# A float32 two-block network on one core: wide projections, features by transposes, low parts by accumulating transfers, attention rows late

## The chip, the cores and the metric

The kernel runs on one core of one Trainium2 chip. Its metric is the device time of one execution in microseconds (us). The engines are named as in the profile: PE (matmuls), PEld (the loading of PE's stationary operand), DVE (elementwise and reductions), ACT (activations and copies), POOL (general purpose; here it could issue transfers) and SP, whose queue issues almost every transfer.

## The reference, cut to what matters

The input is 256 positions of width 1024, float32. The first block has two layers; the second block has two more.

```python
# first block, layer 0: mLSTM mixer, then conv FFN; layer 1: attention, then conv FFN
u = rmsnorm(x, norm_g) @ w_in;  q, k, v, o, gates = split(u)
h = h + (rmsnorm(mlstm(q, k, v, gates)) * sigmoid(o)) @ w_out      # a_w_out
u = rmsnorm(h, g) @ w_up;  c = causal_conv3(u);  val, gate = split(c)
h = h + (silu(gate) * val) @ w_down
h = h + attention(q from h, k and v shared) @ w_o                  # b_w_o
# second block, twice
h = rmsnorm(x, g_pre) * (1 + scale) + shift
u_val, u_gate, g_conv, c_q, c_kv, k_idx, w_idx, g_attn = split(h @ w_in)
y_conv = (silu(layernorm(causal_conv31(u_val * sigmoid(u_gate)))) @ w_pw2) * silu(g_conv)
y_attn = top_k_attention(c_q, c_kv, k_idx, w_idx) * silu(g_attn)
x = x + gate * rmsnorm(concat(y_conv, y_attn) @ w_out, g_post)
```

## The kernel before, in words

Activations lie feature-major in the first block (128 features on the partitions, 256 positions along the row) and row-major in the second block's residual `hm` (two halves of 128 positions, index `t`). Most products are made of high and low parts, both in pages of the kernel's type `F32R`, the high one rounded to it. `split_w` (L525) makes a weight page's high part by a copy on ACT and its low part by a subtraction on DVE. `mm3` (L565) then adds three products: high by high, high by low, low by high. A weight page is 128 x 1024 values, 512 KB; a `Chunk` (L533) is one or two pages. A chunk named in `NATIVE` (L92) is not split: its matmuls run in full float32, which the trace shows as two records each.

`gemm_pair` (L632) computes 256 output features by 256 positions from a chunk of eight slices: 2 x 8 x 3 matmuls of 256 columns. `gemm_sums` (L592) does the same from operands whose high and low parts lie side by side in one page ("rr"): per slice one 512-column product of the weights' high part with both, and one 256-column product of the weights' low part with the high part (`mm2`, L582). The two halves of the PSUM bank are then added. Before the change only the FFN's up projections, from the third chunk on, use it.

The second block's features come from `Head` (L1096). `norm(t)` makes the row statistics and scales the identity matrix by them; `feats(t)` multiplies the rows by that matrix, which scales and transposes them in one full-float32 matmul. ACT evicts eight blocks from PSUM with scale and shift, and ACT and DVE split them.

A layer of the second block (`dsa_layer`, L1186) takes the latents (456 columns), the index scores, the top-k choice (DVE), the four convolution projections `u`, 30 taps on DVE, queries, gates (`w_ga`, `w_gc`), eight heads, then the output rows: `acc` holds the rows of both halves, first the attention's four slices for both halves, then `w_pw2`, then the convolution's four slices, the rest of the norm and the next layer's features, half by half.

The order on every engine is written ahead of time by a planner (`Program.order`, L193). It goes by the order of the program text as priority, with an estimate for each instruction, and lets an engine take a later instruction while an earlier one is not ready. Pages are limited: 24 of type R (split parts), 25 of type F (raw weights and float32 data). An instruction is placed when its pages are free, so the prefetch runs as far ahead as pages allow. An accumulating transfer would be issued by POOL, plain loads by SP; each queue keeps its order.

Of the kernel before, what the change touches and what calls it, by code (L numbers as in the profile page):

```python
# [41 lines left out]
for _n, _c in CONSTS:  # L42
# [5 lines left out]
PAGES = {  # L48
    "R": (1024, F32R, 24),
    "F": (1024, F32, 25),  # L50
    "s": (16, F32, 40),
# [334 lines left out]
def build(ctx, tc, a):  # L386
# [137 lines left out]

    def split_w(raw, n):  # L525
        hi, lo = new("w", n), new("w", n)
        op = act(hi, raw, AF.Copy)
        if hold[0]:
            pg.after(op, hold[0])
        tt(lo, raw, hi.f32, ALU.subtract)  # L530
        return hi, lo

    class Chunk:  # L533


        def __init__(self, dram, kc, mc, k0=0, native=False, cuts=None):
            self.mc, self.kp, self.k0 = mc, 1024 // mc, k0
            self.parts = []
            for k in range(k0, kc, self.kp):
                n = min(self.kp, kc - k) * mc  # L540
                raw = new("raw", n)
                if cuts:
                    hi, lo = new("w", n), new("w", n)
                    for c in cut(cuts, n):
                        load(raw[:, c], dram[:, k * mc + c.start:k * mc + c.stop])
                        act(hi[:, c], raw[:, c], AF.Copy)
                        tt(lo[:, c], raw[:, c], hi[:, c].f32, ALU.subtract)
                    self.parts.append((hi, lo))
                    continue
                load(raw, dram[:, k * mc:k * mc + n])  # L550
                self.parts.append((raw, None) if native else split_w(raw, n))

# [29 lines left out]
    def mm2(out, pairs, start, stop):  # L582
# [6 lines left out]
        pg.add("PE", 2 * (768 / 2.4 + 6), emit, [x for (lh, ll), both in pairs for x in (lh, ll, both)], [out])  # L589


    def gemm_sums(ch, both):  # L592
        out = []
        for b in range(2):
            ps, lo, u = psum(), blk(), blk()
            for k in range(0, 8, 2):
                mm2(ps, [(ch.at(i, b * 128, b * 128 + 128), both[i]) for i in (k, k + 1)], k == 0, k == 6)
            act(lo, ps[:, 256:512], AF.Copy)
            tt(u, ps[:, 0:256], lo, ALU.add)
            out.append(u)  # L600
        return out
# [36 lines left out]
    def half(ps, b):  # L638
        return ps[:, b * S:b * S + S]
# [32 lines left out]

    def scaled(xs, gname, i0):
        out = []
        for k, x in enumerate(xs):
            hi, lo = new("r"), new("r")
# [13 lines left out]


    xs = scaled(xT, None, 0)
# [133 lines left out]
    for j in range(2):  # L826
# [9 lines left out]
        for i in range(2):  # L836
            tp = psum()
            for b in range(2):
                for t in range(2):
                    tr(tp[:, b * S + t * 128:b * S + t * 128 + 128], yt[t * 2 + i][:, b * 128:b * 128 + 128], ident)  # L840
            for b in range(2):
                m, yh, yl = 4 * j + 2 * i + b, new("r"), new("r")
                act(yh, half(tp, b), AF.Copy, scale=ghalf[:, m:m + 1])
                stt(yl, half(tp, b), ghalf[:, m:m + 1], yh.f32, ALU.mult, ALU.subtract)
                ys.append((yh, yl))
# [208 lines left out]
    for h in range(8):  # L1054
        op = psum()
        c = slice((h % 4) * 128, (h % 4) * 128 + 128)
        mm(op[:, 0:256], vt[h // 4][0][:, c], pTs[h][:, 0:256], True, False)
        mm(op[:, 128:256], vt[h // 4][1][:, c], pTs[h][:, 256:384], False, True)
        ys.append(split_x(op[:, 0:256]))
    proj_res("b_w_o", ys, xT)  # L1060


# [33 lines left out]
    class Head:  # L1096
# [89 lines left out]
    def dsa_layer(l, h, last):  # L1186
        hd, xs = heads[l], heads[l].xs
        lw = Chunk(a["w_lat"][l], 8, 456)
        lat = [psum() for _ in range(2)]
# [31 lines left out]
        hold[0] = None  # L1221
        ch = Chunk(a["w_qidx"][l], 2, 512)
        qix = []
# [36 lines left out]
        for j in range(4):  # L1260
            ps = gemm_pair(Chunk(a["w_u"][l * 4 + j], 8, 256, 0, f"u{j}" in NATIVE), xs)
            th, u2, y = blk(), blk(), blk()
# [32 lines left out]
        hold[0] = None  # L1295
        ch = Chunk(a["w_uq"][l], 2, 1024)
        qs = []
# [11 lines left out]
        def gate(i):  # L1309
            nme, j = ("w_ga", "w_gc")[i // 2], i % 2  # L1310
            ps = gemm_pair(Chunk(a[nme][l * 2 + j], 8, 256, 0, f"{nme}{j}" in NATIVE), xs)
            for b in range(2):
# [52 lines left out]
        ch = Chunk(a["w_pw2"][l], 4, 512, 0, "pw" in NATIVE)  # L1365
        for j in range(2):
# [8 lines left out]
        chs = [Chunk(a["w_out_2"][l * 8 + k], 1, 1024, 0, "oc" in NATIVE) for k in range(4)]  # L1375
# [134 lines left out]
```

## Time and profile before

| | us |
|---|---|
| median of three runs | 857.73 (857.71 to 860.17) |
| the profiled execution | 860.24 |
| its span | 858.4 |
| PE busy in the span | 847.8 |

The span is from the first to the last instruction of the profiled execution; 1.8 us of its time lie around the span. A line in the profile names source line, engine, operation, and what is written from what; line 439 is ACT's helper for all activations, 452, 457 and 463 are DVE's, 426 and 430 are plain matmuls and transposes on PE, 573 to 575 the three products of `mm3`, 585 and 587 the two kinds of `mm2`.

### The profile page before, as it was taken

How to read it: one execution, taken by the hardware profiler on the slowest of the kernel's cores; microseconds unless marked ns; L12 is line 12 of the kernel's file. 1: busy time of each engine (PE TensorE's matmuls, PEld its weight loads, DVE VectorE, ACT ScalarE, POOL GpSimd, SP SyncE). 2: the span in 40 equal slices, each digit the busy share in tenths (PEclk: the TensorE clock that was granted, in tenths of full speed). 3: DMA queues.
4: the chain of work that ended last, by engine and by line, in shares of the span. 5: the costliest groups of instructions: out<-in, count | busy, mean ns of one | idle time of the engine just before them, and what ended most of it. 6: DMA issues, size and time to landing. Idle time of an engine off the chain costs nothing.

```text
span 858.4 us, 14510 instructions
## 1 busy us (share of the span) xinstructions
PE 847.8 (99%) x5182; PEld 744.0 (87%) x5182; DVE 751.8 (88%) x1712; ACT 586.5 (68%) x1234; POOL 0.2 (0%) x4
## 2 busy tenths in 40 slices
PE   8999999999999999999999999999999999999997
PEld 8988998999998988889988888888998857998866
DVE  6756899999999899986999999886799998799895
ACT  6845577766666597774787766666953887953883
POOL 0000000000000000000000000000000000000000
PEclk9999999999999999999999999999999999999999
DMA  8985864978877645477377888652430157440201
GB/s 315 408 328 195 295 209 141 316 267 279 263 251 251 198 149 172 142 262 287 123 275 262 297 269 272 195 162 72 162 124 14 52 213 295 133 144 14 59 16 49
DMA packets 50407, 170.19 MB, mean 198 GB/s; under 512 B 5860, under 2 KB 8436, under 8 KB 50336
## 3 DMA queue, kind: packets, MB, share of 16 engines
q1 hardware_dynamic: 50192, 169.28, 57.8%
q8 instruction: 40, 0.66, 0.3%
q14 instruction: 31, 0.25, 0.1%
q10 hardware_dynamic: 144, 0.00, 0.0%
HBM read 167.89 MB, written 1.37 MB: 197 GB/s over the span
## 4 chain that ended last, share of the span: by engine, by line
PE 94%; DVE 3%; ACT 1%; DMA 1%; issue 0%; SPq 0%; DVEq 0%; ACTq 0%
PE ps L573 18%; PE ps L574 17%; PE ps L575 17%; PE ps L585 17%; PE ps L426 14%; PE ps L587 8%; PE ps L430 2%; DVE R L452 2%; DVE F L457 1%; ACT F L439 1%; PE ps L608 1%; DMA F<-in_a_w_v_dram 1%; DVE F L452 0%; PE ps L1276 0%; ACT R L439 0%
## 5 line engine op out<-in xcount | busy, mean ns | idle before, releaser
L452 DVE TENSOR_TENSOR R<-F,R 128x1024 fp32r<-128x1024 f32 (+4 forms) x339 | 325.4, 986 | 24.7 <-ACT R L439 22.2
L573 PE MATMUL ps<-R,R 128*128 128x256 f32 (+3 forms) x1004 | 324.7, 323 | 1.3 <-ACT R L439 1.2
L574 PE MATMUL ps<-R,R 128*128 128x256 f32 (+3 forms) x1004 | 316.8, 316 | 1.3 <-DVE R L452 1.0
L575 PE MATMUL ps<-R,R 128*128 128x256 f32 (+3 forms) x1004 | 316.5, 315 | 0.0
L439 ACT ACTIVATE R<-F 128x1024 fp32r<-128x1024 f32 (+4 forms) x339 | 284.6, 863 | 21.9 <-DVE F L452 16.9
L573 PEld LDWEIGHTS ps<-R,R 128*128 128x128 f32 x1004 | 192.3, 192 | 14.7 <-ACT R L439 2.6
L574 PEld LDWEIGHTS ps<-R,R 128*128 128x128 f32 x1004 | 192.5, 192 | 12.7 <-DVE R L452 2.9
L575 PEld LDWEIGHTS ps<-R,R 128*128 128x128 f32 x1004 | 192.3, 192 | 12.0 <-DVE R L452 0.8
L585 PE MATMUL ps<-R,R 128*128 128x512 f32 x640 | 201.2, 396 | 0.0
L439 ACT ACTIVATE F<-ps 128x256 f32<-128x256 f32 (+4 forms) x269 | 99.9, 393 | 111.6 <-PE ps L587 39.5
L457 DVE SCALAR_TENSOR_TENSOR F<-F,par,F 128x255 f32<-128x255 f32 (+11 forms) x346 | 143.7, 470 | 2.1 <-ACT F L439 1.5
L587 PEld LDWEIGHTS ps<-R,R 128*128 128x128 f32 x640 | 120.1, 188 | 28.7 <-DVE R L452 0.7
L426 PE MATMUL ps<-F,F 128*128 128x256 f32 (+6 forms) x566 | 127.2, 376 | 0.9 <-ACT F L439 0.7
L587 PE MATMUL ps<-R,R 128*128 128x256 f32 x640 | 126.0, 278 | 0.0
L426 PEld LDWEIGHTS ps<-F,F 128*128 128x128 f32 (+2 forms) x566 | 90.1, 190 | 19.6 <-issue 8.2
L585 PEld LDWEIGHTS ps<-R,R 128*128 128x128 f32 x640 | 98.7, 189 | 1.3
L452 DVE TENSOR_TENSOR F<-ps,F 128x256 f32<-128x256 f32 (+2 forms) x152 | 63.6, 432 | 30.6 <-ACT F L439 14.6
L439 ACT ACTIVATE F<-F 128x256 f32<-128x256 f32 (+2 forms) x112 | 43.7, 413 | 47.5 <-DVE F L457 41.1
L457 DVE SCALAR_TENSOR_TENSOR F<-F,F 128x1024 f32<-128x1024 f32 (+1 forms) x53 | 60.3, 1146 | 6.7 <-ACT F L439 6.7
L439 ACT ACTIVATE F<-F,par 128x256 f32<-128x256 f32 x96 | 57.0, 595 | 8.0 <-DVE F L452 7.1
L457 DVE SCALAR_TENSOR_TENSOR F<-F,par 128x255 f32<-128x255 f32 (+1 forms) x86 | 41.0, 480 | 1.0 <-ACT F L439 0.7
L439 ACT ACTIVATE F<-F,s 128x128 f32<-128x128 f32 (+1 forms) x80 | 33.2, 444 | 4.1 <-DVE s L478 3.3
(99 smaller groups left out, 421.9 us busy)
## 6 DMA issues: line engine op xcount, KB each, us to landing
F<-in_f_w_up_dram SPq DMA_DIRECT2D x88, 512.0 KB, 5.3
F<-in_w_ada_dram SPq DMA_DIRECT2D x48, 512.0 KB, 5.0
F<-in_f_w_down_dram SPq DMA_DIRECT2D x44, 512.0 KB, 4.6
F<-in_w_u_dram SPq DMA_DIRECT2D x16, 512.0 KB, 5.2
F<-in_w_out_dram SPq DMA_DIRECT2D x16, 512.0 KB, 3.5
F<-in_a_w_o_dram SPq DMA_DIRECT2D x8, 512.0 KB, 10.1
F<-in_a_w_out_dram SPq DMA_DIRECT2D x8, 512.0 KB, 10.2
F<-in_w_k_dram SPq DMA_DIRECT2D x8, 512.0 KB, 4.6
```

The lines of the kernel that those rows point to most:

```text
L426: pg.add("PE", dur, lambda: nc.tensor.matmul(g(out), g(lhsT), g(rhs), start=start, stop=stop, skip_group_check=not check), [lhsT, rhs], [out])
L430: pg.add("PE", 110.0, lambda: nc.tensor.transpose(g(out), g(x), g(idn)), [x, idn], [out])
L439: nc.scalar.activation(g(out), g(x), func, bias=g(bias), scale=g(scale), **kw)
L452: return pg.add("DVE", ddur(n or x.n), lambda: nc.vector.tensor_tensor(g(out), g(x), g(y), op), [x, y], [out])
L457: nc.vector.scalar_tensor_tensor(g(out), g(x), g(s), g(y), op0, op1, **kw)
L573: nc.tensor.matmul(o, g(lh), g(rh), start=start, stop=False, **kw)
L574: nc.tensor.matmul(o, g(lh), g(rl), start=False, stop=False, **kw)
L575: nc.tensor.matmul(o, g(ll), g(rh), start=False, stop=stop, **kw)
L585: nc.tensor.matmul(g(out), g(lh), g(both), start=start and i == 0, stop=False, skip_group_check=True)
L587: nc.tensor.matmul(g(out[:, 0:256]), g(ll), g(both[:, 0:256]), start=False, stop=stop and i == 1, skip_group_check=True)
L608: nc.tensor.matmul(g(out[e * 64:e * 64 + 64, c]), g(v[s][e]), g(p[e][:, r]), start=s == 0, stop=s == 1, skip_group_check=True)
```

## The change

Pages: R from 24 to 27, F from 25 to 22. The query chunks, the second key chunk and both output projections use the wide form; their operands are made side by side, and an output projection adds both halves of each bank to the residual. `norm` scales the rows themselves in three pieces on DVE, and `feats` transposes them. In the second block `w_gc1` is no longer native, and for `w_gc1`, `pw`, `w_ga0`, `w_gc0` and `u2` the low part is a negated copy of the high part by ACT, to which a transfer issued by POOL adds the raw page. The attention's output rows of the second half stand behind the first half's rows. Gates 2 and 3 are computed one pair of heads earlier. (Adapted calls of `Chunk` are left out below.)

```diff
-    "R": (1024, F32R, 24),
-    "F": (1024, F32, 25),
+    "R": (1024, F32R, 27),
+    "F": (1024, F32, 22),
...
-GATES = (0, 1), (), (2,), (3,), ()
+HSCALE = (0, 256, "D"), (256, 512, "D"), (512, 1024, "D")
+GATES = (0, 1), (2,), (3,), (), ()
...
-NATIVE = {"oa", "u3", "w_ga1", "w_gc1"}
+NATIVE = {"oa", "u3", "w_ga1"}
+BY_DMA = {"w_gc1", "pw", "w_ga0", "w_gc0", "u2"}
+ACCTAIL = 6000.0
...
-    def split_w(raw, n):
+    def split_w(raw, n, by_dma=False):
         hi, lo = new("w", n), new("w", n)
         op = act(hi, raw, AF.Copy)
...
-        tt(lo, raw, hi.f32, ALU.subtract)
+        if by_dma:
+            act(lo, hi.f32, AF.Copy, scale=-1.0)
+            pg.add("POOL", 1100.0, lambda: nc.gpsimd.dma_start(g(lo), g(raw), accum_op=ALU.add), [raw, lo], [lo], tail=ACCTAIL)
+        else:
+            tt(lo, raw, hi.f32, ALU.subtract)
...
+    def gemm_wide(ps, ch, b, both):
+        for k in range(0, 8, 2):
+            mm2(ps, [(ch.at(i, b * 128, b * 128 + 128), both[i]) for i in (k, k + 1)], k == 0, k == 6)
...
-    def gemm_sums(ch, both):
+    def gemm_sums(ch, both, sc=1.0):
         out = []
         for b in range(2):
             ps, lo, u = psum(), blk(), blk()
...
+            gemm_wide(ps, ch, b, both)
+            act(lo, ps[:, 256:512], AF.Copy, scale=sc)
+            if sc == 1.0:
+                tt(u, ps[:, 0:256], lo, ALU.add)
+            else:
+                stt(u, ps[:, 0:256], sc, lo, ALU.mult, ALU.add)
             out.append(u)
...
         for j in range(2):
+            if j or dram == "a_w_q":
+                out += gemm_sums(Chunk(a[dram][j], 8, 256), xboth, sc)
+                continue
...
     def proj_res(dram, xs, h):
         for j in range(4):
-            ps = gemm_pair(Chunk(a[dram][j], 8, 256), xs)
+            ch = Chunk(a[dram][j], 8, 256)
             for b in range(2):
-                m = 2 * j + b
-                tt(h[m], half(ps, b), h[m], ALU.add)
+                m, ps = 2 * j + b, psum()
+                gemm_wide(ps, ch, b, xs)
+                for i in range(2):
+                    tt(h[m], half(ps, i), h[m], ALU.add)
...
         def norm(self, t):
-            self.r[t] = blk()[:, 0:128]
             r = rstd_parts(sq_parts(self.h[t], CUTS, SQBY[t]))
-            ts(self.r[t], ident, r, None, ALU.mult)
+            self.r[t] = new("raw")
+            for c0, c1, e in HSCALE:
+                (by_act if e == "A" else by_dve)(self.r[t][:, c0:c1], self.h[t][:, c0:c1], r)
...
                 for i in range(4):
-                    mm(tp[:, i * 128:i * 128 + 128], self.h[t][:, q * 512 + i * 128:q * 512 + i * 128 + 128], self.r[t], True, True)
+                    tr(tp[:, i * 128:i * 128 + 128], self.r[t][:, q * 512 + i * 128:q * 512 + i * 128 + 128], ident)
...
-        for k in range(4, 8):
-            ch = Chunk(a["w_out_2"][l * 8 + k], 1, 1024, 0, "oa" in NATIVE)
-            for t in range(2):
+        oas = [Chunk(a["w_out_2"][l * 8 + k], 1, 1024, 0, "oa") for k in range(4, 8)]
+        def attention_rows(t):
+            for k in range(4, 8):
                 for c0, c1, y in acc[t]:
-                    mm_tm(y, mix[k], ch.at(0, c0, c1), t, k == 4, False)
+                    mm_tm(y, mix[k], oas[k - 4].at(0, c0, c1), t, k == 4, False)
+        attention_rows(0)
...
         for t in range(2):
             q2, z = [], [blk() for _ in range(4)]
+            if t:
+                attention_rows(1)
             for c0, c1, y in acc[t]:
```

## Rows read from the trace of the kernel before

**Rows 1.** The page, busy time of each engine, share of the span, instructions.

```profile
PE 847.8 (99%) x5182; PEld 744.0 (87%) x5182; DVE 751.8 (88%) x1712; ACT 586.5 (68%) x1234; POOL 0.2 (0%) x4
```

**Rows 2.** The page, chain that ended last: its shares by engine.

```profile
PE 94%; DVE 3%; ACT 1%; DMA 1%; issue 0%; SPq 0%; DVEq 0%; ACTq 0%
```

**Rows 3.** Busy time by stretch: stretch, length, busy us per engine, clock, DMA share, GB/s.

```profile
140.00:280.00 140.00, 139.92 (x919) 127.39 (x920) 132.34 (x230) 92.94 (x157) 0.00 (x0) 1.00 0.80 264
410.00:590.00 180.00, 180.00 (x1001) 155.45 (x1000) 164.66 (x291) 126.18 (x221) 0.00 (x0) 1.00 0.67 222
590.00:730.00 140.00, 138.43 (x837) 116.12 (x835) 124.72 (x345) 100.09 (x244) 0.00 (x0) 1.00 0.40 140
690.00:710.00 20.00, 19.51 (x79) 10.32 (x78) 19.83 (x48) 18.52 (x41) 0.00 (x0) 1.00 0.62 220
730.00:850.00 120.00, 119.60 (x753) 102.60 (x753) 106.67 (x307) 80.53 (x196) 0.00 (x0) 1.00 0.21 65
```

**Rows 4.** Timeline of PE where the second block's layers meet: start, duration, instruction.

```profile
708.83 0.39 PE L574 MATMUL ps<-R,R 128*128 128x256 f32 x1 [0.49 <-DVE R L452]
...
725.44 2.05 PE L426 MATMUL ps<-F,F 128*128 128x128 f32 x16 [0.15 <-DVE s L464]
727.99 0.47 PE L573 MATMUL ps<-R,R 128*128 128x456 f32 x1 [0.49 <-ACT R L439]
```

**Rows 5.** Timeline of PE in a run of `mm3`: first and 35th of 35.

```profile
299.91 0.28 PE L573 MATMUL ps<-R,R 128*128 128x256 f32 x1
...
303.99 0.28 PE L574 MATMUL ps<-R,R 128*128 128x256 f32 x1
```

**Rows 6.** Timeline of PE in a wide chunk of an FFN, three groups apart.

```profile
239.90 0.39 PE L587 MATMUL ps<-R,R 128*128 128x256 f32 x2
...
241.99 0.40 PE L587 MATMUL ps<-R,R 128*128 128x256 f32 x2
```

**Rows 7.** Timeline of PE: feature products, native matmuls, and eight transposes with the next matmul.

```profile
604.43 1.95 PE L426 MATMUL ps<-F,F 128*128 128x128 f32 x16
606.13 0.46 PE L573 MATMUL ps<-R,R 128*128 128x456 f32 x1
...
606.84 2.32 PE L426 MATMUL ps<-F,F 128*128 128x256 f32 x10
...
431.14 1.09 PE L430 MATMUL ps<-con,F 128*128 128x128 f32 x8
431.99 0.48 PE L585 MATMUL ps<-R,R 128*128 128x512 f32 x1
```

**Rows 8.** Groups by shape, whole span: count, busy us, mean ns, idle before.

```profile
L452 DVE TENSOR_TENSOR R<-F,R 128x1024 fp32r<-128x1024 f32 x230 | 277.9, 1220 | 15.9 <-ACT R L439 15.1 <-DMA F<-in_w_out_dram 0.5
L439 ACT ACTIVATE R<-F 128x1024 fp32r<-128x1024 f32 x230 | 237.1, 1051 | 1.5 <-PE ps L575 1.5
L452 DVE TENSOR_TENSOR F<-ps,F 128x256 f32<-128x256 f32 x144 | 58.9, 422 | 28.4 <-ACT F L439 14.6 <-PE ps L575 12.1 <-PE ps L608 0.3
L463 DVE TENSOR_SCALAR F<-F,s 128x256 f32<-128x256 f32 x8 | 2.8, 349 | 0.0
L463 DVE TENSOR_SCALAR F<-F,s 128x128 f32<-128x128 f32 x8 | 2.3, 283 | 0.0
```

**Rows 9.** Groups by shape, 630 to 700 us: split pages.

```profile
L439 ACT ACTIVATE R<-F 128x1024 fp32r<-128x1024 f32 x7 | 7.4, 1052 | 0.0
L452 DVE TENSOR_TENSOR R<-F,R 128x1024 fp32r<-128x1024 f32 x1 | 1.2, 1212 | 0.0
```

**Rows 10.** The same, 700 to 712 us.

```profile
L452 DVE TENSOR_TENSOR R<-F,R 128x1024 fp32r<-128x1024 f32 x6 | 7.2, 1228 | 0.0
```

**Rows 11.** Transfers by source: count, KB, median us from issue to landing.

```profile
F<-in_w_out_dram SPq DMA_DIRECT2D x16, 512.0 KB, 3.5
F<-in_a_w_out_dram SPq DMA_DIRECT2D x8, 512.0 KB, 10.2
```

**Rows 12.** Waits of SP's queue: us in total, times, longest.

```profile
SPq L490 <- DVE R L452: 343.2, 173, 11.5
```

More of the change, by code (lines that the diff above doesn't have):

```diff
@@ L529, in split_w, with __init__ @@
             pg.after(op, hold[0])
-        tt(lo, raw, hi.f32, ALU.subtract)
+        if by_dma:
[3 more added lines that the diff above has]
+            tt(lo, raw, hi.f32, ALU.subtract)
         return hi, lo
     class Chunk:
-        def __init__(self, dram, kc, mc, k0=0, native=False, cuts=None):
+        def __init__(self, dram, kc, mc, k0=0, name=None, cuts=None):
             self.mc, self.kp, self.k0 = mc, 1024 // mc, k0
@@ L550, in __init__ @@
                 load(raw, dram[:, k * mc:k * mc + n])
-                self.parts.append((raw, None) if native else split_w(raw, n))
+                self.parts.append((raw, None) if name in NATIVE else split_w(raw, n, name in BY_DMA))
         def at(self, k, c0, c1):
@@ L595, in gemm_sums @@
             ps, lo, u = psum(), blk(), blk()
[L596 to L599, printed above, removed]
+            gemm_wide(ps, ch, b, both)
[4 more added lines that the diff above has]
+                stt(u, ps[:, 0:256], sc, lo, ALU.mult, ALU.add)
             out.append(u)
@@ L671, in sum_sq, with scaled @@
         return st[:, :S]
-    def scaled(xs, gname, i0):
+    def scaled(xs, gname, i0, into=None):
         out = []
         for k, x in enumerate(xs):
-            hi, lo = new("r"), new("r")
+            if into is None:
+                hi, lo = new("r"), new("r")
+            else:
+                into.append(new("rr"))
+                hi, lo = into[k][:, 0:256], into[k][:, 256:512]
             gk = pcols(gname, i0 + k) if gname else an[:, k:k + 1]
@@ L687, in build @@
         mm(zacc[:, 0:256], zero[:, 0:128], zero, True, True)
-    xs = scaled(xT, None, 0)
+    xboth = []
+    xs = scaled(xT, None, 0, xboth)
     def qk(dram, sc):
@@ L841, in build @@
             for b in range(2):
-                m, yh, yl = 4 * j + 2 * i + b, new("r"), new("r")
+                m, both = 4 * j + 2 * i + b, new("rr")
+                yh, yl = both[:, 0:256], both[:, 256:512]
                 act(yh, half(tp, b), AF.Copy, scale=ghalf[:, m:m + 1])
                 stt(yl, half(tp, b), ghalf[:, m:m + 1], yh.f32, ALU.mult, ALU.subtract)
-                ys.append((yh, yl))
+                ys.append(both)
     def proj_res(dram, xs, h):
         for j in range(4):
-            ps = gemm_pair(Chunk(a[dram][j], 8, 256), xs)
+            ch = Chunk(a[dram][j], 8, 256)
             for b in range(2):
-                m = 2 * j + b
-                tt(h[m], half(ps, b), h[m], ALU.add)
+                m, ps = 2 * j + b, psum()
+                gemm_wide(ps, ch, b, xs)
+                for i in range(2):
+                    tt(h[m], half(ps, i), h[m], ALU.add)
     proj_res("a_w_out", ys, xT)
@@ L1058, in build @@
         mm(op[:, 128:256], vt[h // 4][1][:, c], pTs[h][:, 256:384], False, True)
-        ys.append(split_x(op[:, 0:256]))
+        both = new("rr")
+        act(both[:, 0:256], op[:, 0:256], AF.Copy)
+        tt(both[:, 256:512], op[:, 0:256], both[:, 0:256].f32, ALU.subtract)
+        ys.append(both)
     proj_res("b_w_o", ys, xT)
@@ L1187, in dsa_layer @@
         hd, xs = heads[l], heads[l].xs
[L1188 removed]
+        lw = Chunk(a["w_lat"][l], 8, 456, 0, "lat")
         lat = [psum() for _ in range(2)]
@@ L1221, in dsa_layer @@
         hold[0] = None
-        ch = Chunk(a["w_qidx"][l], 2, 512)
+        ch = Chunk(a["w_qidx"][l], 2, 512, 0, "qi")
         qix = []
@@ L1260, in dsa_layer @@
         for j in range(4):
-            ps = gemm_pair(Chunk(a["w_u"][l * 4 + j], 8, 256, 0, f"u{j}" in NATIVE), xs)
+            ps = gemm_pair(Chunk(a["w_u"][l * 4 + j], 8, 256, 0, f"u{j}"), xs)
             th, u2, y = blk(), blk(), blk()
@@ L1295, in dsa_layer @@
         hold[0] = None
-        ch = Chunk(a["w_uq"][l], 2, 1024)
+        ch = Chunk(a["w_uq"][l], 2, 1024, 0, "uq")
         qs = []
@@ L1310, in gate @@
             nme, j = ("w_ga", "w_gc")[i // 2], i % 2
-            ps = gemm_pair(Chunk(a[nme][l * 2 + j], 8, 256, 0, f"{nme}{j}" in NATIVE), xs)
+            ps = gemm_pair(Chunk(a[nme][l * 2 + j], 8, 256, 0, f"{nme}{j}"), xs)
             for b in range(2):
@@ L1374, in dsa_layer @@
                 mix[2 * j + b] = (None, None, t) if "oc" in NATIVE else split_x(t)
-        chs = [Chunk(a["w_out_2"][l * 8 + k], 1, 1024, 0, "oc" in NATIVE) for k in range(4)]
+        chs = [Chunk(a["w_out_2"][l * 8 + k], 1, 1024, 0, "oc") for k in range(4)]
         for t in range(2):
             q2, z = [], [blk() for _ in range(4)]
+            if t:
+                attention_rows(1)
             for c0, c1, y in acc[t]:
```

2 lines of the change are left out of this document (1 added, 1 removed).

## The prediction

> **What bounds the kernel now.** First the busy table of the page: PE is busy for 847.8 of 858.4 us, DVE for 88%, ACT for 68%, POOL for nothing [rows 1]. A busy PE need not be the bound, so next the chain of waits: 94% of the chain that ended last is PE, 3% DVE [rows 2]. Then the busy times by stretch [rows 3]: in the first conv-FFN (140 to 280 us) PE idles 0.08 us, in the second (410 to 590 us) not at all; in the second block's first layer (590 to 730 us) 1.57 us, most of it where the layer ends (690 to 710 us: PE 19.51 of 20, DVE 19.83, ACT 18.52); in the second layer 0.40 us. The timeline of PE at the change of layers names who ends those holes: a low part from DVE at 708.8, the row statistics at 725.4, the high parts from ACT at 728.0 us [rows 4]. So nearly all of the time is matmuls issued back to back: a column of PE work that goes away shortens the run by itself, and work that is only moved to or from DVE and ACT counts where PE would have waited for it.
>
> **The change, part by part.**
>
> *Wide projections.* Eleven weight chunks (three of the query/key chunks, four each of the two output projections) go from `gemm_pair` to `gemm_wide`. A pair chunk is 2 blocks x 8 slices x 3 products of 256 columns = 48 matmuls; starts in such a run lie 0.12 us apart (299.91 to 303.99 us, 34 steps) [rows 5], so 5.76 us. A wide chunk has as many columns, in 32 instructions: per block four groups of two 512-column and two 256-column products. A group takes 0.697 us (239.90 to 241.99 us, three groups) [rows 6], eight groups 5.57 us. Gain 0.19 us a chunk, 2.1 us for eleven. What it adds: 16 adds from PSUM and six combining operations on DVE, 22 x 0.42 us [rows 8] = 9.3 us at most, beside FFN stretches where DVE idles 7.7 us (140 to 280) and 15.3 us (410 to 590) [rows 3]. Hidden as it stands; if that cover were gone for the adds behind the very last block, two of them, it would be 0.8 us at each of two stage ends. I take 0.5 us in all.
>
> *Features by transposes.* Each layer has 8 feature products for each of two row halves: 32 in all. Eight of them, full-precision matmuls in 16 records, hold PE from 604.43 until the next matmul at 606.13: 1.70 us. Eight transposes hold it from 431.14 to 431.99: 0.85 us [rows 7]. The difference, 0.85 us, four times: 3.4 us. Before it, one 128-column scaling of the identity (0.28 us) becomes scalings of 256, 256 and 512 columns: 0.35, 0.35 and, with 0.066 us per 128 further columns, some 0.48 us [rows 8], on DVE. The first two pieces are there 0.70 us after the statistics and the four transposes of the first bank 0.2 us later; before, 0.28 plus 0.85 us. So the evictions on ACT start no later, and the second bank follows at once. Lower end of the gain 1.7 us (the second half of each layer waits for its rows anyway), upper end 3.4. I take 3.4.
>
> *Low parts by transfers.* Five chunks of two pages a layer (`u2`, `w_ga0`, `w_gc0`, `w_gc1`, `pw`). For four of them DVE loses its subtraction, 16 pages x 1.22 us = 19.5 us; ACT gets the negated copy, 20 x 1.05 = 21.0 us [rows 8], and POOL issues 20 accumulating transfers. `w_gc1` was native: 16 products of two 256-column records each; such records come 0.216 us apart ((2.32 - 0.38)/9) [rows 7], so 6.91 us; as three-product pairs 5.76 us. Gain 1.15 us a layer, 2.3 us; its split adds four more ACT copies, 4.2 us. ACT's 12.6 us more a layer stand against 39.9 and 39.5 us of idle time in the two layers [rows 3], so I cost them at nothing; without that cover they are 25.2 us.
>
> The transfer itself no row shows. The nearest are loads of the same 512 KB: landed after 3.5 us in a quiet stretch, after 10.2 us in the busy start [rows 11]. As the destination is read as well, I take 3.5 us as lower and twice 10.2 = 20.4 us as upper end, and expect 5 to 7 us, close to the quiet rows, since these layers move little. Whether it shows depends on the lead. Between 630 and 700 us ACT made seven high parts and DVE one low part; six low parts come only after 700 us, when the taps are done [rows 9, 10]. So DVE, not the data, made those pages late; a transfer issued behind a copy at 636 to 651 us would have some 50 us. Hence no wait. Behind a late transfer on POOL only later transfers queue; raw pages stay taken until it lands, and the loads on SP wait for raw pages already (173 waits for DVE's subtractions, 343 us) [rows 12]. I cost this at nothing: the load queue runs ahead of PE.
>
> The Trainium skill (DMA: Bandwidth & Descriptors, Anatomy of one DMA, SWDGE path) gives about 2.0 us plus the bytes at 436 GB/s for a transfer issued by GpSimd. As an estimate from that page, 512 KB would be 3.2 us and the sum would stay as it is; no run here shows one.
>
> *Attention rows late, gates earlier, pages.* Eight native 512-column products per layer for the second row half now stand behind the first half's rows. No work is removed. Before, PE waited 0.49 us at 708.8 for a low part and 0.15 and 0.49 us at 725 to 728 us for the first half's statistics and features [rows 4]; now it has these products then. But after the second half's rows only the first half's latent products are left to cover the second half's features. The first layer's idle time is 1.57 us and the three waits are 1.13 of it [rows 3, 4]; I take 1.0 us as regained, bounds minus 2 (a new hole at the second half) and plus 1.6 us. Gates moved one head earlier do the same work. Three pages move from type F to R: nothing as long as loads stay ahead.
>
> **The sum.** 2.1 + 3.4 + 2.3 = 7.8 us less PE work, 1.0 us of waits regained, 0.5 us lost to the added adds: 8.3 us. The profiled execution took 860.24 us (span 858.4 and 1.8 around it): 851.9. The median of the three runs is 857.73, 2.5 us under the profiled one, so 849.4 us there.
>
> **The rivals.**
>
> A. *Low parts arrive too late; slower.* Place: the wait of PE for a low part written by a transfer. If a transfer takes 10.2 us rather than about 6, every page that PE reaches on schedule costs 4.2 us. One such page in each layer eats the gain (849.4 + 8.4 = 857.8), two make 866. It decides from two pages a layer, or from transfers of over 12 us if they are served one at a time (ten in a layer of some 128 us). For it: no transfer of this kind in the trace, ten a layer on one queue. Against it: 50 us of lead, DMA that moves 140 GB/s in the layer where it moves 264 in the first FFN [rows 3]. The Trainium skill speaks for it too (SBUF, State Buffer; Who interferes with whom): GpSimd's descriptor writing is locked out while DVE runs a one-source operation on both ports. The change adds 12 such scalings; no run here shows such a lock. From the rows, a scaling lasts 0.28 to 0.48 us, so even a lock for one or two delays a transfer by less than 1 us: it doesn't decide A.
>
> B. *ACT becomes the bound where the layer ends.* In 690 to 710 us ACT has 1.5 us left [rows 3]. If four negated copies (4.2 us) fall there, PE waits 2.7 us a layer: 854.8. For it: ACT makes high parts there already, some of the seven of [rows 9]. Against it: raw data is there earlier, and DVE's relief lets the norm start earlier.
>
> C. *The second half's features stay bound by their chain.* The gain of the transposes halves (1.7 us) and the late rows leave a hole in place of a gain (1.0 us regained, 0.6 lost): 849.4 + 3.3 = 852.7. For it: after the second half's rows PE has only some 5 us of latent products. Against it: the same pattern at 600 us, before the first layer, shows no wait.
>
> D. *Loads come late.* Three fewer F pages shorten the lead by three loads, about 6 us at one 512 KB load in 2 us (264 GB/s). If the lead is no longer than that in an FFN, some 7 us of starvation: 857. Against it: PE waits nowhere for an FFN load now.
>
> **How the numbers follow.** Forecast 0.60 (own range 846 to 853), C 0.12, B 0.10, D 0.06, A 0.12. A measurement tells 0.3%, 2.6 us, from no change: faster is under 855.2, slower over 860.3. Faster: 0.60 + 0.12, and about half of B and a third of D, 0.79. Same: the other half of B, most of D, a little of A: 0.11. Slower: the rest of A, 0.10. The range goes down to 844.5 (all of the 1.57 and 0.40 us of idle time regained and no loss to the adds makes 848.0; the rest is for the median of the runs, which lies 2.5 us from the profiled one) and up to 859, which leaves out A's heavier cases.
>
> **What would show it.** PE's busy time lower by 7 to 8 us at the same shares; 32 fewer pairs of 128-column full-precision records and 32 more transposes; 5.57 us chunks in the output projections; about 32 fewer native 256-column records a layer. Wrong would be: a wait of PE for a low part released by a transfer (A), ACT at its limit before the layer's end with PE waiting for it (B), PE idle for over 1 us before the second half's features (C), a wait for a load (D).

## The result and the profile after

The changed kernel is slower: 866.32 us (median of 6 runs, 865.76 to 868.68), against 858.7 us for the kernel before in the same comparison (857.71 to 860.4). The ratio is 1.0091, 95% interval 1.0072 to 1.0109. The forecast was 849.4, and 844.5 to 859 the range. The profiled execution, the slowest of the six, took 868.68 us (span 866.9), 8.4 us more than that of before.

The page of the changed kernel: busy time of each engine, the chain that ended last by engine, the transfers' queue (packets, MB, share of 16 engines) and the transfers (count, KB, median us to landing).

```profile
PE 843.2 (97%) x5006; PEld 732.1 (84%) x5006; DVE 742.1 (86%) x1726; ACT 603.1 (70%) x1254; POOL 17.6 (2%) x24
...
PE 85%; DMA 5%; issue 4%; ACT 3%; DVE 2%; POOL 0%; SPq 0%; DVEq 0%; POOLq 0%; ACTq 0%
...
q0 software_dynamic: 2880, 10.49, 6.2%
...
R<-F POOLq DMA_DIRECT2D x20, 512.0 KB, 7.6
```

PE is busy 4.6 us less than in [rows 1] in a span 8.5 us longer: the work fell, and waits came. In [rows 2] PE had 94% of the chain and DMA 1%; now DMA has 5% and "issue" 4%. The timeline of PE where it waited longest (start, duration, instruction, and in brackets the wait and who ended it):

```profile
656.03 1.19 PE L429 MATMUL ps<-F,con 128*128 128x256 f32 x2 [5.28 <-DMA F<-zscr]
729.32 0.47 PE L582 MATMUL ps<-R,R 128*128 128x456 f32 x1 [1.50 <-ACT R L442]
738.86 1.54 PE L433 MATMUL ps<-con,F 128*128 128x128 f32 x6 [4.26 <-DVE F L466]
792.35 0.67 PE L429 MATMUL ps<-F,con 128*128 128x256 f32 x2 [1.42 <-DMA F<-zscr]
```

The first and the last are the convolution mean: `zs`, the sums of the taps, goes to DRAM and comes back shifted. The middle two are the second layer's features, where [rows 4] showed 0.49 us and less: the first half's, whose evictions (copies out of PSUM) come from ACT, and the second half's, whose scaled rows come from DVE. Busy time by stretch of the changed kernel (columns as in [rows 3]) shows what follows each hole:

```profile
650.00:655.00 5.00, 0.75 (x7) 0.54 (x5) 4.18 (x11) 4.97 (x8) 0.86 (x1) 1.00 0.31 88
655.00:662.00 7.00, 5.97 (x20) 5.38 (x21) 4.74 (x13) 0.70 (x3) 0.86 (x1) 0.53 0.87 186
...
737.00:744.00 7.00, 5.14 (x18) 4.61 (x19) 4.12 (x11) 6.83 (x24) 0.86 (x1) 0.52 0.78 188
```

PE was busy 0.75 of 5 us, and then ran 7 us at a mean granted clock of 0.53: nearly all of it at 1.2 in place of 2.4 GHz. At 737 us it is the same. The loss counts only while PE works: from 656.03 to 662.5 us PE is all busy at a mean of 0.52, from 738.86 to 744.5 at 0.53. That is 3.1 and 2.7 us.

The account of the 8.5 us of span: PE idles 13.1 us more (866.9 - 843.2 against 858.4 - 847.8) and is busy 4.6 us less. Of the added idle time 11.3 us are the waits in the four rows above (12.46 against 1.13 in [rows 4]). Of its busy time PE lost 5.8 us to the clock; before, 1.7 us (45 to 60 us, mean clock 0.89) and up to 1.6 in the first 20 us (0.91), where it also waits for loads. So PE's work itself fell by 7.1 to 8.7 us, around the 7.8 of the forecast. The low clock in the first 60 us of before is no part of the change: e10 below, which changes only the second block's features and their place, has 1.00 in both stretches.

Where the first hole comes from, by the chain of waits of the changed kernel (start, us, what):

```profile
631.12 0.01 POOLq L536
631.13 14.43 DMA R<-F
...
645.64 0.41 ACT F L442 x2
646.05 5.50 DMA zscr<-F
...
651.60 4.29 DMA F<-zscr
655.89 0.14 issue
656.03 1.19 PE ps L429 x2
```

A transfer of a low part takes 14.43 us from issue to landing. The copy of `zs` waits for a page until it has landed, its write takes 5.50 us, its return 4.29. The DMA view of 620 to 650 us, first of the changed kernel, then of the one before:

```profile
DMA packets 2239, 7.83 MB, mean 261 GB/s; under 512 B 252, under 2 KB 367, under 8 KB 2235
q0 software_dynamic: 864, 3.15, 53.5%
q1 hardware_dynamic: 1371, 4.64, 44.2%
...
R<-F POOLq DMA_DIRECT2D x5, 512.0 KB, 12.7
F<-in_w_out_dram SPq DMA_DIRECT2D x4, 512.0 KB, 9.6
zscr<-F SPq DMA_DIRECT2D x1, 143.5 KB, 5.5
```

```profile
q1 hardware_dynamic: 864, 2.77, 27.4%
...
F<-in_w_out_dram SPq DMA_DIRECT2D x3, 512.0 KB, 4.5
zscr<-F SPq DMA_DIRECT2D x1, 143.5 KB, 2.0
```

The DMA engines are full (53.5% + 44.2%) where they were a quarter busy (27.4%), and the loads and the write in that stretch take twice as long and more. It holds more loads too, 4.64 MB against 2.77; e3 and e18 below tell what of it is the transfers. In the trace the five transfers were issued 2.0 to 2.8 us apart from 624 us on; they landed 9.9, 10.9, 12.7, 14.4 and 16.3 us later, 3.6 to 3.9 us apart. The Trainium skill (DMA: Bandwidth & Descriptors, Issuing engines are not separate DMA queues) says that transfers of all issuing engines run on the same 16 DMA engines and interleave; these rows agree.

### The profile page after: what moved, and what is told of

Its sections match the earlier page's. It is cut to its first block, busy times and chain, and to the rows that moved or that the text cites. A ratio compares the mean times of both kernels' runs of the same rounds, so it can differ in the third digit from the quotient of the medians.

```text
span 866.9 us, 14260 instructions
## 1 busy us (share of the span) xinstructions
PE 843.2 (97%) x5006; PEld 732.1 (84%) x5006; DVE 742.1 (86%) x1726; ACT 603.1 (70%) x1254; POOL 17.6 (2%) x24
## 3 DMA queue, kind: packets, MB, share of 16 engines
q0 software_dynamic: 2880, 10.49, 6.2%
## 4 chain that ended last, share of the span: by engine, by line
PE 85%; DMA 5%; issue 4%; ACT 3%; DVE 2%; POOL 0%; SPq 0%; DVEq 0%; POOLq 0%; ACTq 0%
PE ps L594 21%; PE ps L582 13%; PE ps L583 13%; PE ps L584 13%; PE ps L429 12%; PE ps L596 10%; PE ps L433 2%; DMA R<-F 2%; ACT F L442 1%; ACT R L442 1%; DMA zscr<-F 1%; DMA F<-zscr 1%; DVE R L455 1%; DVE F L460 1%; PE ps L623 1%
## 5 line engine op out<-in xcount | busy, mean ns | idle before, releaser
L442 ACT ACTIVATE R<-F 128x1024 fp32r<-128x1024 f32 (+4 forms) x343 | 289.1, 866 | 21.8 <-DVE F L455 13.1
L582 PE MATMUL ps<-R,R 128*128 128x256 f32 (+3 forms) x860 | 285.4, 332 | 2.3 <-ACT R L442 2.3
L584 PE MATMUL ps<-R,R 128*128 128x256 f32 (+3 forms) x860 | 275.0, 320 | 0.8 <-DVE R L455 0.7
L583 PE MATMUL ps<-R,R 128*128 128x256 f32 (+3 forms) x860 | 274.9, 320 | 0.7 <-DVE R L455 0.6
L594 PE MATMUL ps<-R,R 128*128 128x512 f32 x816 | 256.9, 396 | 0.0
L596 PEld LDWEIGHTS ps<-R,R 128*128 128x128 f32 x816 | 153.3, 188 | 36.1
L442 ACT ACTIVATE F<-ps 128x256 f32<-128x256 f32 (+5 forms) x269 | 100.5, 395 | 114.4 <-PE ps L596 44.3
L582 PEld LDWEIGHTS ps<-R,R 128*128 128x128 f32 x860 | 164.3, 191 | 17.8 <-ACT R L442 4.1
L583 PEld LDWEIGHTS ps<-R,R 128*128 128x128 f32 x860 | 164.5, 191 | 12.8 <-DVE R L455 2.1
L584 PEld LDWEIGHTS ps<-R,R 128*128 128x128 f32 x860 | 164.1, 191 | 12.9 <-DVE R L455 1.7
L596 PE MATMUL ps<-R,R 128*128 128x256 f32 x816 | 160.4, 278 | 0.0
L460 DVE SCALAR_TENSOR_TENSOR F<-F,par,F 128x255 f32<-128x255 f32 (+20 forms) x364 | 151.8, 468 | 3.5 <-ACT F L442 2.9
L594 PEld LDWEIGHTS ps<-R,R 128*128 128x128 f32 x816 | 125.4, 189 | 1.1
L429 PE MATMUL ps<-F,F 128*128 128x256 f32 (+6 forms) x434 | 106.2, 398 | 0.9 <-ACT F L442 0.8
L429 PEld LDWEIGHTS ps<-F,F 128*128 128x128 f32 (+2 forms) x434 | 71.5, 194 | 16.0 <-issue 5.9
L433 PE MATMUL ps<-con,F 128*128 128x128 f32 (+2 forms) x190 | 32.1, 281 | 4.5 <-DVE F L466 4.5
L433 PEld LDWEIGHTS ps<-con,F 128*128 128x128 f32 (+2 forms) x190 | 24.0, 145 | 14.1 <-DVE F L466 5.5
```

The source lines that it names most:

```text
L429: pg.add("PE", dur, lambda: nc.tensor.matmul(g(out), g(lhsT), g(rhs), start=start, stop=stop, skip_group_check=not check), [lhsT, rhs], [out])
L433: pg.add("PE", 110.0, lambda: nc.tensor.transpose(g(out), g(x), g(idn)), [x, idn], [out])
L442: nc.scalar.activation(g(out), g(x), func, bias=g(bias), scale=g(scale), **kw)
L460: nc.vector.scalar_tensor_tensor(g(out), g(x), g(s), g(y), op0, op1, **kw)
L582: nc.tensor.matmul(o, g(lh), g(rh), start=start, stop=False, **kw)
L583: nc.tensor.matmul(o, g(lh), g(rl), start=False, stop=False, **kw)
```

## The experiments

Ratios are to the kernel before, timed beside each group of runs; 0.001 is 0.86 us. Two theories at first. T: the transfers cost the time. L: the attention's late output rows leave the second half's features uncovered.

**e1: the rows of both halves early again.**

```diff
-        attention_rows(0)
+        for k in range(4, 8):
+            for t in range(2):
+                for c0, c1, y in acc[t]:
+                    mm_tm(y, mix[k], oas[k - 4].at(0, c0, c1), t, k == 4, False)
...
-            if t:
-                attention_rows(1)
```

> The changed kernel with one part undone: the attention's output rows of both halves stand ahead of the first half's rows again. Everything else as in the changed kernel (866.3 us). Theory L (late rows make the hole where the layers meet): the 1.66 and 4.43 us that PE waits for the first and second half's features at 727 and 734 us, and the 6.8 us at half clock behind them (3.4 us lost), go; in exchange come back waits of 1 to 2 us as the kernel before had there: 858 to 860 us. Theory T (the accumulating transfers and their copies on ACT make both holes): 864 to 867 us, with PE still waiting over 3 us for the second half's features.

871.32 us, ratio 1.0151 (1.0130 to 1.0171): missed by both, and 5 us worse than with the late rows. PE's waits from 590 us on (us in total, times, longest):

```profile
PE ps L429 <- DMA F<-zscr: 8.2, 2, 5.5
PE ps L433 <- DVE F L466: 4.2, 1, 4.2
```

The wait for the second half's features is still there with the rows early, so L is out. The two means cost 8.2 us of waiting in place of 6.7. The profiled executions are only 1.4 us apart (e1's fastest, the changed kernel's slowest), so where the rest of the 5 us went isn't shown. (The expectations give the waits 0.1 to 0.2 us longer than the timelines do.)

**e2: no transfers. e3: the same transfers, short** (64 of 1024 columns, so the low parts are incomplete).

```diff
-BY_DMA = {"w_gc1", "pw", "w_ga0", "w_gc0", "u2"}
+BY_DMA = set()                                    # e2
...
-nc.gpsimd.dma_start(g(lo), g(raw), accum_op=ALU.add)
+nc.gpsimd.dma_start(g(lo[:, 0:64]), g(raw[:, 0:64]), accum_op=ALU.add)   # e3
```

> The changed kernel with every low part made by DVE's subtraction again (no transfer by POOL; w_gc1 stays split). Theory T: the 5.4 us that PE waits near 650 us for the convolution mean's round trip, the 3.4 us lost at half clock behind it and the 1.6 us of the second layer go, at the price of 20 subtractions of 1.22 us on DVE, of which up to 2 us a layer show: 856 to 860 us; no wait of ACT or DVE for a transfer's page. Theory L: the hole near 650 us stays, 865 to 868 us. If DVE is what the transfers were needed for: 862 us or more with PE waiting for DVE's low parts at the end of the layer.

> The changed kernel in the same order of instructions, but each accumulating transfer moves 64 of the 1024 columns, so the low parts of the ten pages a layer are not completed: the cost of the transfers' length alone. Theory T in the narrow form (one transfer holds its page for 10 to 16 us because each takes some 3.8 us of the queue, and the page's next user waits): the hole near 650 us shrinks to under 1 us and the half clock behind it goes, 855 to 858 us, while the hole near 734 us stays. If the order or ACT's added copies made that hole: 864 to 867 us.

e2: 862.81 us, 1.0045 (1.0027 to 1.0062). PE doesn't wait for the mean, as T has it, but T's time is missed by 2.8 us: where the layers meet PE waits 4.1 us for DVE's scalings, the longest at 722.01 us (2.41), and over the second block 1.1 us for DVE's low parts. That fits the third expectation in part; that the subtractions are what delays the scalings isn't shown.

e3: 858.88 us, 0.9995 (0.9984 to 1.0005). With every engine's order the same, the length of the transfers costs 8.2 us by the ratios (7.4 by the medians), and PE doesn't wait for the mean. But e3 is still no faster than before, so there is a second cause.

**e4: e1 and e2 together, and `w_gc1` native again.**

```diff
-NATIVE = {"oa", "u3", "w_ga1"}
+NATIVE = {"oa", "u3", "w_ga1", "w_gc1"}
```

> The changed kernel with both undone (rows of both halves early, no transfers, w_gc1 native again): the wide projections, the features by transposes, the earlier gates and the page counts are left. By the terms of the prediction 2.1 and 3.4 us less PE work than the kernel before: 852 to 855 us. If the pages or the longer features chain cost what they gain: 857 to 860 us.

864.14 us, 1.0064 (1.0049 to 1.0079): missed by both. With wide projections, transposed features, gates and page counts left, PE still waits 4.25 us where the layers meet.

Theory O came from ACT's timeline there. Before, the second half's output statistic (the rows `s<-`) stood ahead of the first half's evictions (`F<-ps,mod`):

```profile
726.26 0.30 ACT L439 ACTIVATE s<-s,s 128x1 f32<-128x1 f32 x1
726.59 0.20 ACT L439 ACTIVATE s<-s 128x1 f32<-128x1 f32 x1
726.70 0.79 ACT L439 ACTIVATE F<-ps,mod 128x128 f32<-128x128 f32 x2
```

In the changed kernel it stands behind all of them, and the scaling that PE waits for until 738.86 follows from it:

```profile
728.01 0.81 ACT L442 ACTIVATE F<-ps,mod 128x128 f32<-128x128 f32 x2
...
731.47 0.79 ACT L442 ACTIVATE F<-ps,mod 128x128 f32<-128x128 f32 x2
732.29 0.42 ACT L442 ACTIVATE R<-F 128x256 fp32r<-128x256 f32 x1
732.61 0.28 ACT L442 ACTIVATE s<-s,s 128x1 f32<-128x1 f32 x1
732.93 0.20 ACT L442 ACTIVATE s<-s 128x1 f32<-128x1 f32 x1
733.03 2.94 ACT L442 ACTIVATE R<-F 128x1024 fp32r<-128x1024 f32 x3
```

The planner lets ACT take what is ready first; features that are ready sooner put 4.6 us of evictions ahead of the other half's chain. In e7 below, where nothing else is changed, the first eviction starts at 725.91 us, 0.79 us sooner than before.

**e5: the changed kernel, first half's features behind the second half's statistic in the program. e6: the changed kernel with matrix features. e7: the kernel before with transposed features alone. e8: with the wide projections alone** (the last by undoing the other parts).

```diff
             rr = rstd_parts(q2)
+            if t and not last:
+                heads[l + 1].feats(0)
...
                 heads[l + 1].norm(t)
-                heads[l + 1].feats(t)
+                if t:
+                    heads[l + 1].feats(t)         # e5
...
-ts(self.r[t], ident, r, None, ALU.mult)
+by_dve(self.r[t][:, c0:c1], self.h[t][:, c0:c1], r)   # e7, three pieces; e6 the reverse
...
-ps = gemm_pair(Chunk(a[dram][j], 8, 256), xs)
+gemm_wide(ps, ch, b, xs)                          # e8, and the query and key chunks
```

> The changed kernel with one thing moved: the first half's features of the next layer stand behind the second half's row statistics in the program, so that ACT takes those two small instructions ahead of the first half's evictions. Theory O (transposes are done sooner than the matrix products were, so ACT starts the first half's 4.6 us of evictions before the second half's statistics are ready, and those wait behind them): PE's waits of 1.66 and 4.43 us near 730 us shrink to under 2 us in sum, and the 6.8 us at half clock behind them go: 858 to 861 us, with the hole near 650 us still there. If the scaling of whole rows or the extra ACT copies make that hole: 865 to 868 us.

> The changed kernel with the features as matrix products with the scaled identity again; wide projections, transfers, late rows and pages stay. Theory O: the second half's features wait under 1 us near 730 us, no half clock there; 3.4 us more PE work: 859 to 862 us. If late rows or transfers made that hole: 868 to 871 us.

> The kernel before with the features by transposes of scaled rows as its only edit. Theory O: slower, although PE has 3.4 us less to do: a wait of about 4 us for the second half's features and 3.4 us lost at half clock: 861 to 865 us. The prediction's sum: 855 us.

> The kernel before with the wide projections as its only edit (eleven chunks). The prediction's sum: 2.1 us less, 856 to 857 us, with the second block beginning some 2 us earlier. If the added adds and combining operations on DVE show at the ends of the projections: 858 to 860 us.

e5: 866.60 us, 1.0084 (1.0062 to 1.0107). The wait of 4.3 us is gone, but O's time is missed by 5.6 us: PE waits 4.78 us for the first layer's mean and 3.44 for the second's, until 789.25 us, with half clock behind both.

e6: 867.53 us, 1.0089 (1.0071 to 1.0107), missed. The second half's features wait 0.58 us, as O has it, but ahead of them PE waits 2.76 us, until 737.43, for the transposes of the first half's queries, and 2.45 and 2.48 us near 650 us. While the transfers are there, mending one hole doesn't shorten the run.

e7: 865.42 us, 1.0067 (1.0050 to 1.0084), 0.4 us above O's range: the transposed features alone lose 5.8 us, with a wait of 4.26 us.

e8: 857.32 us, 0.9975 (0.9966 to 0.9985): 2.1 us gained, the term of the sum.

**e9: e4 with e5's order. e10: e7 with it. e11: e5 with e3's short transfers (low parts incomplete). e12: e5 with the transfer's cost in the plan as measured.**

```diff
-ACCTAIL = 6000.0
+ACCTAIL = 1500.0
...
-            pg.add("POOL", 1100.0, ...
+            pg.add("POOL", 3850.0, ...            # e12
```

> The changed kernel without transfers, with the attention's rows of both halves early and w_gc1 native, and with the first half's features behind the second half's row statistics in the program. Theory O (the hole at the change of layers is ACT's order: the first half's evictions run ahead of the second half's statistic): both parts of the PE work saved so far are kept, 857.3 with the wide projections alone less 3.4 for the transposes, so 852 to 855, and PE waits less than 2.5 us at the change of layers. Rival (the hole is set by the second half's rows, whatever ACT does first): it stays at 4 us and more with a half-clock stretch behind it, 860 to 864, as without the changed order (864.14).

> The kernel before with nothing but the transposed features, and the first half's features behind the second half's statistics. Theory O: 858.5 less 3.4, 854 to 857, against 865.4 with the transposed features in the old order. Rival (the transposes themselves cost the time, for example by the clock behind them): 861 to 866, with the wait of 4.4 us or a half-clock stretch still there.

> The changed kernel with the statistics first, and each accumulating transfer cut to 64 of 1024 columns, so that the low parts are incomplete. If the length of the transfers and ACT's order at the change of layers are the two causes and there is no third, PE has neither the hole at 650 us nor that of 4.4 us at 734 us: 850 to 854, near the forecast. If another wait takes their place (the layer norm's round trip in the second layer, 785 us): 857 and more.

> The changed kernel with the statistics first, where the order is worked out with 3.85 us of POOL and 1.5 us of landing for a transfer, instead of 1.1 and 6.0: what the profile shows of queued ones. If the loss comes from an order that takes queued transfers for short ones, the waits at the layer norms (650 and 785 us) shrink to under 2 us: 854 to 860. If the length of the transfers costs the time whatever the order: 864 to 868, with those waits of 3 to 5 us.

e9: 858.53 us, 1.0004 (0.9995 to 1.0014), 5.2 us better than e4 by the ratios. e10: 860.52 us, 1.0024 (1.0011 to 1.0036), 3.7 us better than e7. In both the wait of 4.3 us is gone, and without the transfers the order is worth 4 to 5 us: so much of O holds. But O's times, 852 to 855 and 854 to 857, are missed: e9 is 2.5 us slower than e8 by the ratios, e10 2.1 us slower than before. Even in that order the transposes lose about 2 us. PE at the second layer's first latents, e9 and then e8:

```profile
724.94 0.47 PE L582 MATMUL ps<-R,R 128*128 128x456 f32 x1 [1.90 <-ACT R L442]
```

```profile
725.00 0.47 PE L582 MATMUL ps<-R,R 128*128 128x456 f32 x1 [0.56 <-ACT R L442]
```

The start is the same within 0.06 us, though e9 began the second block's features 1.0 us later (592.94 against 591.93 us; its clock was at 0.91 in the first 20 us, that of e8 at 1.00). From there to this wait e9 took 2.4 us less than e8, as the three groups of transposes should save (3 x 0.85); 1.3 of it is waited away here, for ACT's evictions. In e9 a stretch at half clock follows the wait, in e8 none (columns as in [rows 3], e9 and then e8):

```profile
720.00:740.00 20.00, 17.73 (x82) 14.55 (x81) 16.61 (x42) 19.24 (x56) 0.00 (x0) 0.91 0.49 166
```

```profile
720.00:740.00 20.00, 19.35 (x108) 16.63 (x107) 15.37 (x40) 18.96 (x61) 0.00 (x0) 1.00 0.41 134
```

20 x 0.09 = 1.8 us.

e11: 855.33 us, 0.9966 (0.9955 to 0.9977): with short transfers and the order mended the longest wait left after the first 20 us is this one, 1.91 us; missed by 1.3 us.

e12: 867.03 us, 1.0096 (1.0074 to 1.0117): an order that knows the transfers' cost loses as much, with 4.2 us of waiting for each layer's mean. So the plan's estimate isn't the cause.

**e13: the changed kernel, where the copy of `zs` has a page of its own.**

```diff
+    "Z": (512, F32, 1),
...
+    "z": ("Z", 4, 512),
...
-        zs, zm = wide(), blk()
+        zs, zm = new("z", 384), blk()
```

> The changed kernel, the same order on every engine, but the copy of the tap sums that goes through DRAM has a page of its own in each layer. Theory Z (that copy waits for a raw page which a late transfer still reads): the hole of 5.4 us at 650 us shrinks to under 2 us and its half-clock stretch goes, 5.4 plus 3.4 less up to 2: 858 to 862. Rival (the round trip itself is slow beside the transfers, or another page is as late): the hole stays over 4 us, 865 to 868.

865.99 us, 1.0082 (1.0062 to 1.0102), as the rival has it: theory Z fell. Chain of waits of e13:

```profile
642.16 0.91 DVE F L462 x2
...
643.10 7.69 DMA zscr<-Z
...
650.85 4.35 DMA F<-zscr
...
655.33 1.19 PE ps L431 x2
```

The write starts 2.95 us sooner and takes 7.69 us instead of 5.50. PE waits 4.64 us in place of 5.28. The page was only the last lock: the backlog of the DMA engines sets the hole.

**e14: the kernel before with wide projections and `w_gc1` split by ACT and DVE. e15: the same with `w_gc1`'s low part alone by transfers, two a layer, gates and page counts as changed. e16: e9 with half of the evictions on DVE.**

```diff
-BY_DMA = {"w_gc1", "pw", "w_ga0", "w_gc0", "u2"}
+BY_DMA = {"w_gc1"}                                # e15
...
-XACT = (1, 1, 1, 1), (1, 1, 1, 1)
+XACT = (1, 0, 1, 0), (1, 0, 1, 0)                 # e16
```

> The kernel before with the wide projections and with w_gc1 split into high and low parts by ACT and DVE, nothing else. If DVE can take four more subtractions of 1.22 us in each layer: 857.3 less 2.3, 854 to 856. If DVE is the bound in the second block's layers: its 4.9 us a layer come back as waits of PE for low parts, 858 to 866.

> As the wide projections alone, with w_gc1 split and its low part alone made by transfers (two a layer in place of ten), with the page counts and the gates of the change. Theory Q (it is the queue of transfers that costs, not the single one): 857.3 less 2.3, 854 to 857, no hole at 650 us. Rival (a transfer costs as soon as it holds a raw page for 5 us and more): a wait at the layer norm of 2 us and more, 859 to 864.

> The kernel with both wide projections and transposed features, statistics first (858.53), where DVE evicts four of the eight feature blocks of each half in place of ACT. If ACT's work between the first half's statistics and its last eviction is what PE waits for at 724.9 us (1.90 us): the wait falls under 1 us and the half-clock stretch behind it goes, 854 to 857. If DVE is as full there: the wait stays or grows, 858 to 862.

e14: 863.26 us, 1.0055 (1.0036 to 1.0075): with DVE making them, the low parts of one more chunk a layer cost 6.9 us against e8; PE waits for low and high parts at 706, 707, 837 and 838 us.

e15: 860.72 us, 1.0015 (1.0002 to 1.0028), the rival's time without the rival's wait: PE doesn't wait for the mean, and the transfers land after 5.0 us in the first layer and 7.3 in the second. But the first half's latents, which began at 722.92 us, 2.1 us ahead of e8, ended in a wait of 2.31 us for the transposes of their queries, and the second half's features came only behind that. ACT's timeline has the order of theory O again.

e16: 862.99 us, 1.0049 (1.0029 to 1.0068): missed; 1.55 and 3.10 us of waiting. Moving evictions to DVE is no way out.

**e17: e15 with e5's order. e18: the changed kernel with plain copies in place of the adding transfers.**

```diff
-nc.gpsimd.dma_start(g(lo), g(raw), accum_op=ALU.add)
+nc.gpsimd.dma_start(g(lo), g(raw))                # e18
```

> The kernel with wide projections, matrix-product features and w_gc1's low part by two transfers a layer (860.72), with nothing changed but that the first half's features stand behind the second half's row statistics. Its trace showed 722.9 us for the start of the second layer's latents, 2.1 us ahead of the wide projections alone, and then 2.31 us of waiting behind ACT's evictions and 6.8 us at half clock. Theory O: these two go, 860.7 less 2.3 and 3.4: 854 to 856, which would beat both kernels. Rival (the time is set by the chain of rows, norm and statistics there, and the earlier arrival is waited away in any order): 857 to 861.

> The changed kernel, the same order, with each accumulating transfer replaced by a plain copy of the same 512 KB (the low parts are then wrong: they hold the raw pages). If adding to the destination is what makes queued transfers land 3.6 to 3.9 us apart: they land about 2 us apart as issued, the hole at 650 us falls under 2 us, 858 to 861. If any copy of 512 KB from page to page takes that long: landings as far apart as before, 865 to 868.

e17: 855.53 us, 0.9962 (0.9949 to 0.9976), as O has it, 4.6 us better than e15 by the ratios, and faster than both kernels; from e8 its interval doesn't set it apart. PE's waits where the layers meet (us in total, times, longest), e15 and then e17:

```profile
PE ps L433 <- DVE F L466: 2.3, 1, 2.3
PE ps L429 <- DVE F L466: 0.5, 1, 0.5
PE ps L582 <- ACT R L442: 0.5, 1, 0.5
```

```profile
PE ps L582 <- ACT R L442: 0.9, 1, 0.9
```

And the stretch behind them, by the columns of [rows 3], e15 and then e17:

```profile
730.00:738.00 8.00, 7.02 (x27) 6.13 (x28) 6.91 (x12) 7.42 (x19) 0.00 (x0) 0.57 0.64 208
```

```profile
730.00:738.00 8.00, 8.00 (x47) 7.34 (x46) 4.50 (x10) 7.43 (x24) 0.00 (x0) 1.00 0.39 133
```

e18: 859.78 us, 1.0006 (0.9995 to 1.0017). The same bytes as plain copies take half of the DMA engines' time (whole span, and 620 to 650 us):

```profile
q0 software_dynamic: 2880, 10.49, 3.3%
```

```profile
R<-F POOLq DMA_DIRECT2D x7, 512.0 KB, 7.6
F<-in_w_out_dram SPq DMA_DIRECT2D x5, 512.0 KB, 7.0
zscr<-F SPq DMA_DIRECT2D x1, 143.5 KB, 2.5
```

Of the five issued 2.0 to 2.8 us apart, as in the changed kernel, the first two landed 3.8 us apart and the rest 2.6; PE waited 0.3 us for the mean. So it is the adding: 7.3 us by the ratios.

## Why the prediction was wrong

The step that failed first is the price of the transfers: "I cost this at nothing: the load queue runs ahead of PE." The duration was bounded (3.5 to 20.4 us, measured 4.8 alone and 12.7 in the queue), but only their readers were looked at. No low part was late, which is what rival A had feared. What the transfers took was the DMA engines' time: 6.2% of the span, 53.7 us over 20, 2.7 us each with all 16 engines; and five come within 9 us (624 to 633) beside the output weights' loads. The victim was a small round trip through DRAM that PE waits for and that the prediction didn't name. "DMA that moves 140 GB/s in the layer" was a mean over 140 us; the stretch of 30 us that mattered became full. e3 shows 8.2 us for it, e18 that 7.3 of it is the adding. Rival A had the right part, and nearly the right time (866) by luck, since it named another place; its chance was 0.12.

The second is in *Features by transposes*: "So the evictions on ACT start no later, and the second bank follows at once." True, and it is the trouble: in the planned order they go ahead of the second half's statistic, and the second half's features come 4.3 us late. In place of 3.4 us gained, 5.8 are lost (e7). Rival C saw the chain but only as a halved gain. With the order mended it is still a loss of about 2 us (e10): the latents wait for ACT's evictions either way. The term's 0.85 us a group is right as PE work, but it became waiting and time at half clock (in e9 1.3 and 1.8 us where the layers meet).

Third, no price was put on a hole beyond its own length. Behind the 5.28 us at 656 us and the 4.26 at 739 the clock took 3.1 and 2.7 us more, behind the 1.90 us of e9 1.8. The price doesn't follow the length: behind the 2.31 us of e15 it is 3.0 (7.02 us busy at 0.57), behind a wait of 5.46 us in e1 1.5 (656 to 660 us, 3.59 us busy at 0.57), and behind the 1.50 and 1.42 us of the changed kernel the clock stayed at 1.00.

Fourth, the late rows. "I take 1.0 us as regained" rests on "now it has these products then", and it had not:

```profile
714.37 1.02 PE L429 MATMUL ps<-F,F 128*128 128x512 f32 x2
726.51 1.31 PE L433 MATMUL ps<-con,F 128*128 128x128 f32 x8 [0.21 <-DVE F L466]
```

The last of the attention's native 512-column products stand at 714 us, ahead of both halves' convolution rows, which run without a break until 726: the planner let PE take products that stand later in the program before them. So the first half's features wait 0.21 and 1.50 us in the changed kernel, and 0.22 and 1.49 in e4 with the rows early.

What held: the wide projections, 2.1 us forecast and 2.1 measured (e8; interval 1.3 to 2.9). The 1.15 us a layer of `w_gc1`: in e15 PE reached the second layer's latents 2.1 us ahead of e8, and 0.5 of that it had where the second block's features begin (591.46 against 591.93 us). That leaves 1.6 us for the layer, with the gates and pages changed as well. But the run is shorter only in the right order and with two transfers a layer; by DVE it loses (e14). With the transfers there, undoing the late rows costs 5 us (e1), but by the waits above this isn't a figure for the rows alone; they weren't tried without the other parts. (The gates stand one pair of heads earlier, not one head; nothing rests on it.) That ACT had room over a layer was right; where the layers meet, its order decides.

Why e16 and e6 wait where they do was read from their timelines only; it isn't settled further.

## What to carry to other kernels

Cost a new transfer as DMA-engine time in the 30 us where it runs, not by its own latency, and look for whoever else needs those engines there, small round trips through DRAM first. Before counting a faster step as gain, find what the next engine will do with the earlier data: here 0.8 us sooner put 4.6 us of evictions ahead of the chain that the other half needed. Where PE is nearly full, a wait can cost more than its length by the clock behind it (1.8 us behind 1.90 in e9, 3.0 behind 2.31 in e15), or nothing (behind 1.50 in the changed kernel).

## What was not expected of the hardware

An adding transfer of 512 KB between pages took 4.8 us alone (median of three, 605 to 620 us) and 3.6 to 3.9 us of spacing in a queue beside loads; a plain copy by the same queue 2.9 us alone (605 to 623 us of e18) and 2.6 us of spacing, 3.8 between the first two. In engine time it is 6.2% against 3.3% of the span for the same 10.49 MB. The estimate of 3.2 us from the Trainium skill (DMA: Bandwidth & Descriptors, Anatomy of one DMA, SWDGE path) is 0.3 us above the plain copy; the adding one took 1.6 us longer than it.
